# Four gated-merge blocks beside the last mixer head, another handover from the up- to the down-projection, and the last rows' Newton steps on VectorE

## The chip, the cores and the metric

The kernel runs on one core of a Trainium2 chip. The metric is the device time of one execution in microseconds (us). Engines are named as in the profile: PE is the matmul engine (TensorE), PEld its weight load, DVE is VectorE, ACT is ScalarE, POOL is GpSimd, SP issues the DMAs.

## The reference: one transformer-like layer for two request groups

A prompt of 1024 tokens and 8 samples of 16 new tokens (1152 tokens together, float32, model width 1024) pass one layer. Three mixers A (sliding-window attention), B (gated linear recurrence, 4 heads) and C (gated DeltaNet, 4 heads) are merged with gates; a feed-forward of width 2816 follows.

```python
offsets = [int(o) for o in np.cumsum(IN_SPLITS)[:-1]]
aq, ak, av, bq, bf, bi, bg, cqkv, cz, cb, ca, gt = jnp.split(x @ w_in, offsets, axis=-1)
...
o_b, new_hgrn = run_chunks(gla_chunk, s_hgrn.astype(F32), (q_b, k_b, v_b, log_f))
o_b = merge_heads(rms_norm_gated(o_b, hgrn_w, heads(bg, B_VAL_DIM)))
...
gates = jax.nn.sigmoid(gt.reshape(bsz, t, N_BRANCH, D_MODEL))
w_ba, w_bb, w_bc = jnp.split(w_branch, [A_WIDTH, A_WIDTH + B_WIDTH], axis=0)
mix = gates[:, :, 0] * (o_a @ w_ba) + gates[:, :, 1] * (o_b @ w_bb) + gates[:, :, 2] * (o_c @ w_bc)
x = layer_norm(ALPHA * x + mix @ w_out, ln1_g, ln1_b)

up, new_ffn_conv = causal_dwconv(x @ w_up, buf_ffn, f_conv_w)
gate, val = jnp.split(up + f_conv_b, 2, axis=-1)
x = layer_norm(ALPHA * x + (jax.nn.silu(gate) * val) @ w_down, ln2_g, ln2_b)
```

`causal_dwconv` is a convolution over three tokens in each channel; `rms_norm_gated` divides a head's output by its root mean square, multiplies by a weight and by silu of a gate z.

## The kernel before

**Numbers and tiles.** Tokens lie in three row blocks n = 0, 1, 2 of 384 (`NW`); block 2 holds the last 256 prompt tokens and the 128 sample tokens. A matrix product keeps both operands as a high part (a CAST to the matmul's reduced float32, written fp32r in the profile) and a low part (the rest, one DVE subtraction), and sums three products: high x high, high x low, low x high. So each weight tile costs one load by SP, one ACT CAST and one DVE subtraction (`prep`, `pair`, `prep_step`), and each product tile three matmuls, all issued from `mm` at L108. `block` makes one 128 x 384 output from `kt` tiles of the contraction, and then calls its eviction.

**What sets the order.** The program is written as one sequence, with generators beside it: `beside(gen)` enters one, `tick()` inside the matmul loops steps those whose count has run down, a `yield k` waits k ticks, and `drain()` ticks until none is left. The compiler schedules the emitted instructions engine by engine, by the order of emission and by priorities, and may move them by its own estimate; `keep_in_program_order` and `load_in_turn` bind an instruction to its place. Each engine, and SP's list of DMA issues, then runs its list in order. Tiles come from pools with a number of buffers for each tag; a new tile waits until the old one's readers are done.

**The end of the mixers and the merge.** The 24 groups of mixer work (head, row block) run as generators beside the matmuls. The last is head 3 of B with n = 2: `b_finish` computes a mean square `so`, `rsqrt` makes its inverse root on DVE by an integer guess and three Newton steps (L319 to L327, 2 + 9 instructions), and `finish_group` multiplies the head's output oT by it (L703), transposes its three pieces on PE, multiplies with the weight and z into the tile sq (L709), and stores that to DRAM as d_o. `load_o` reads d_o again and splits it into o high and low (L1478, L1479). The merge multiplies d_o of each branch with its rows of w_branch; `branch_ev` multiplies by the gates and adds into `mix` (L1517, L1518). Branches 2 and 0 run in a queue `Q` beside the mixers. Branch 1 (mixer B) is last: `whl_pair` fetches the weights of the output rows m = 0..3 into two whl buffers, and two more pairs go into wres buffers (raw in wraw). Before, `drain()` stands ahead of all of this, and a loop over n and m then makes the 24 blocks of branch 1, each with `kt=4`, 12 matmuls.

**The up-projection.** 22 pairs of weight columns, a gate and a value column block each (`Pair`). For pairs 2 to 21 the 2 x 2 pattern (two halves of the contraction) x (row blocks 0 and 1) is made by a Strassen-like scheme: seven products over sums of x and of the weights, where `x_sums` builds the four sums of x in four tiles ts. `put` brings a product into xp, `conv` applies the three taps, and the result goes to DRAM as d_gu. Row block 2 is made by plain blocks (`gate_rest`, `behind`). The last transposes of each pair (tile l, `tail`) give the convolution's new state.

**The down-projection.** `prep_step` is one of 66 steps: for n = 0 one weight row block (wdr, CAST L1957, subtraction L1958), and the features of one k: two loads from d_gu (gr), their product (L1962), CAST (L1965) and subtraction (L1966) into gd. The contraction of 22 is done in two halves of 11 k for each n; each step is 18 matmuls of 512 columns into six PSUM banks. `residual` loads the normalised rows into nine tiles yac, times g plus b of the first layer norm (L1943, L1944); `put_sum` adds each half into yac (L2054), `last_ln` does the final layer norm. For the last 128 rows it runs on DVE, with `rsqrt_act`, in which the nine Newton operations are ACT instructions (L1993 to L1996).

The pools: wp holds wraw and whl (2 buffers each, 8 and 16 KB), s0 the 48 tiles of x high and low, xs the sums ts; dp, which is opened after all of these are closed, holds the down-projection's tiles.

## Time and profile before

| what | us |
|---|---|
| three runs | 2266.27, 2268.82, 2265.26 |
| their median | 2266.27 |
| the profiled execution, in all | 2266.73 |
| its span on the profile's page | 2264.9 |

The page gives the busy time of each engine and its share of the span; a digit of the lines by slices is the busy share of one fortieth of the span in tenths. The table of waits counts idle time of one engine by the operation and tile that waited and by what ended the wait: total, times, longest. A row of the timeline is a group of like instructions: start, length, engine, line, operation, out<-in, shape, count, and in brackets the idle time ahead of it with its releaser. A row by stretches has its window and length, then the busy time of PE, PEld, DVE, ACT and POOL, the granted PE clock, the share of the DMA engines and GB/s. The page's lines on the DMA queues give packets, MB and a share of the time of the core's 16 DMA engines; one queue carries nearly everything:

```profile
q1 hardware_dynamic: 261200, 218.06, 31.1%
```

### The profile page before, as it was taken

The numbers are of one execution on the slowest core, as the hardware profiler recorded it, in microseconds if no ns is written. First come the engines' busy times: TensorE is split into PE (matmuls) and PEld (weight loads), VectorE is DVE, ScalarE is ACT, GpSimd is POOL, SyncE is SP. The second block draws the span as 40 slices with busy tenths as digits, with TensorE's granted clock in tenths as the row PEclk, the third lists the DMA queues.
The fourth block names the chain that finished last, engine by engine and source line by source line (L and its number), as shares of the span: only waits on it lengthen the run. The fifth ranks groups of instructions, "written<-read, shape, count | busy, mean of one in ns | idle before, by whom it ended". The sixth has DMA issues, their size and how long they took to land.

```text
span 2264.9 us, 35159 instructions
## 1 busy us (share of the span) xinstructions
PE 2178.8 (96%) x12759; PEld 2030.1 (90%) x12759; DVE 1530.2 (68%) x4246; ACT 982.7 (43%) x2309; POOL 1.3 (0%) x9
## 2 busy tenths in 40 slices
PE   7999999999999999999999899999999999689998
PEld 7998889999999999999989888899999999567886
DVE  7367556666765657767878786877777777674444
ACT  4356434344345346355433333544545445231234
POOL 0000000000000000000000000000000000000000
PEclk9999999999999999999999999999999999899999
DMA  5121231222222221312354541232323232674421
GB/s 139 44 76 56 86 102 48 74 73 65 69 78 57 76 60 52 94 42 64 119 157 137 164 151 75 70 102 94 102 97 108 92 97 76 224 233 128 155 98 56
DMA packets 261373, 220.30 MB, mean 97 GB/s; under 512 B 38810, under 2 KB 250688, under 8 KB 261184
## 3 DMA queue, kind: packets, MB, share of 16 engines
q1 hardware_dynamic: 261200, 218.06, 31.1%
q8 instruction: 100, 1.64, 0.3%
q14 instruction: 73, 0.60, 0.1%
HBM read 152.86 MB, written 66.06 MB: 97 GB/s over the span
## 4 chain that ended last, share of the span: by engine, by line
PE 85%; DVE 5%; DMA 5%; ACT 3%; issue 1%; SPq 1%; DVEq 0%; ACTq 0%
PE psg L108 72%; PE psp L108 5%; PE psch L108 4%; DMA gr<-d_gu 2%; PE psp L148 2%; PE psch L148 1%; PE psms L108 1%; PE psms L148 1%; DMA xp<-d_o 1%; SPq L111 1%; DVE gr L1962 0%; DVE yac L1944 0%; DVE gd L1966 0%; ACT L1223 0%; DVE yac L1943 0%
## 5 line engine op out<-in xcount | busy, mean ns | idle before, releaser
L108 PE MATMUL psg<-hh,whl 128*128 128x384 f32 x2976 | 809.0, 344 | 0.8 <-ACT qf L436 0.7
L108 PEld LDWEIGHTS psg<-hh,whl 128*128 128x128 f32 x2976 | 535.6, 188 | 15.4 <-issue 8.6
L108 PE MATMUL psg<-hl,whl 128*128 128x384 f32 x1488 | 508.5, 342 | 0.0
L108 PE MATMUL psg<-wd,gd 128*128 128x512 f32 x1188 | 277.0, 396 | 30.9 <-ACT gd L1965 11.2
L108 PEld LDWEIGHTS psg<-wd,gd 128*128 128x128 f32 x1188 | 227.1, 192 | 80.6 <-ACT gd L1965 11.4
L108 PEld LDWEIGHTS psg<-hl,whl 128*128 128x128 f32 x1488 | 280.1, 188 | 4.3 <-issue 2.6
L108 PE MATMUL psg<-x1h,w 128*128 128x384 f32 x672 | 182.0, 340 | 0.0
L108 PE MATMUL psg<-x1h,whl 128*128 128x384 f32 x640 | 172.7, 339 | 2.8 <-ACT whl L212 1.2
L108 PE MATMUL psg<-o,whl 128*128 128x384 f32 x720 | 142.8, 349 | 6.6 <-ACT o L1478 2.6
L108 PEld LDWEIGHTS psg<-o,whl 128*128 128x128 f32 x720 | 127.3, 194 | 9.8 <-ACT o L1478 3.2
L108 PEld LDWEIGHTS psg<-x1h,w 128*128 128x128 f32 x672 | 122.9, 188 | 1.0
L108 PEld LDWEIGHTS psg<-x1h,whl 128*128 128x128 f32 x640 | 116.9, 189 | 4.9 <-ACT whl L212 1.9
L108 PE MATMUL psg<-x1l,w 128*128 128x384 f32 x336 | 113.5, 338 | 0.0
L213 DVE TENSOR_TENSOR whl<-wraw,whl 128x1024 fp32r<-128x1024 f32 (+1 forms) x82 | 91.5, 1117 | 31.9 <-ACT whl L212 30.8
L108 PE MATMUL psg<-x1l,whl 128*128 128x384 f32 x320 | 108.2, 338 | 0.0
L108 PE MATMUL psg<-ts,w 128*128 128x384 f32 x576 | 105.8, 334 | 0.0
L108 PEld LDWEIGHTS psg<-ts,w 128*128 128x128 f32 x576 | 100.6, 188 | 0.0
L1962 DVE TENSOR_TENSOR gr<-gr 128x384 f32<-128x384 f32 x66 | 36.7, 557 | 92.7 <-DMA gr<-d_gu 92.2
L212 ACT CAST whl<-wraw 128x1024 fp32r<-128x1024 f32 (+1 forms) x82 | 79.0, 964 | 36.8 <-PE psg L108 34.4
L108 PE MATMUL psg<-wres,mixh 128*128 128x512 f32 x288 | 92.5, 395 | 0.0
L1965 ACT CAST gd<-gr 128x384 fp32r<-128x384 f32 x66 | 33.8, 512 | 129.5 <-PE psg L108 78.3
L1445 ACT ACTIVATE ga<-psg 128x384 f32<-128x384 f32 x72 | 35.4, 491 | 97.6 <-PE psg L108 80.0
(505 smaller groups left out, 3829.1 us busy)
## 6 DMA issues: line engine op xcount, KB each, us to landing
wraw<-in_w_in_dram SPq DMA_DIRECT2D x58, 512.0 KB
gr<-d_gu SPq DMA_DIRECT2D x132, 192.0 KB
d_g<-ga SPq DMA_DIRECT2D x72, 192.0 KB
wraw<-in_w_up_dram SPq DMA_DIRECT2D x24, 512.0 KB
wdr<-in_w_down_dram SPq DMA_DIRECT2D x22, 512.0 KB
wr<-in_w_up_dram SPq DMA_DIRECT2D x20, 512.0 KB
acc<-d_g SPq DMA_DIRECT2D x48, 192.0 KB
d_gu<-ga SPq DMA_DIRECT2D x44, 192.0 KB
```

The lines of the kernel that those rows point to most:

```text
L108: PE.matmul(out, lhsT, rhs, start=start, stop=stop)
L111: nc.sync.dma_start(out=out, in_=in_)
L148: PE.transpose(out, in_, ident[:n, :n])
L212: S.copy(hl[:, 0, :kt, :cols], raw[:, :kt, :cols])
L213: V.tensor_sub(hl[:, 1, :kt, :cols], raw[:, :kt, :cols], hl[:, 0, :kt, :cols].bitcast(F32))
L1445: S.activation(g, ps, AF.Tanh, scale=0.5)
L1962: V.tensor_mul(raw[:, 0], raw[:, 0], raw[:, 1])
L1965: S.copy(g[:, 0], raw)
```

## The change

**Part 1: the merge beside the last head's close.** The program no longer drains ahead of branch 1. It ticks until the last group has computed its mean square (`ended`), prepares the two whl pairs, runs the four blocks m = 0..3 of n = 0, and only then drains. `finish_group` waits 10 ticks in place of 2 for this last group, and its first transpose keeps its place in the program. The loop leaves out the four blocks done; the gate tiles fetched ahead are those of m = 4..6.

```diff
-    def finish_group(oT, fac, wcol, z2, out):
+    def finish_group(oT, fac, wcol, z2, out, behind=False):
 
         V.tensor_mul(u3(oT), u3(oT), bc(fac, 3))
-        yield 2
+        yield 10 if behind else 2
         ps = psum("ms")
         for i in range(3):
-            tr(ps[:, i * P:(i + 1) * P], oT[:, i * P:(i + 1) * P])
+            t = PE.transpose(ps[:, i * P:(i + 1) * P], oT[:, i * P:(i + 1) * P], ident)
+            if behind and i == 0:
+                tc.keep_in_program_order(t)
...
-    drain()
+    while not ended[0]:
+        tick()
...
     whl_pair(2)
+
+    oh, ol, _ = parts[1]
+    for m in range(4):
+        block(wb[m], oh, ol, 0, branch_ev(1, m), kt=4)
+    drain()
     mix_ctx.close()
...
-    for m in range(3):
+    for m in range(4, 7):
         gate_ahead[1, m, 0] = load_gate(1, m, 0)
...
+            if n == 0 and i < 4:
+                continue
```

PE's list at the end of branch 0, before: the last matmuls of branch 0 (onto whl_14385), the transposes of the last head's oT, and the first matmuls of branch 1 (onto whl_14439).

```order
L108 MATMUL psg_14526<-o_13769,whl_14385 128x384
L108 MATMUL psg_14526<-o_13770,whl_14385 128x384
L108 MATMUL psg_14526<-o_13769,whl_14385 128x384
L148 MATMUL psms_14348<-call,oT_14211 128x128 x3
L108 MATMUL psg_14601<-o_14463,whl_14439 128x384
L108 MATMUL psg_14601<-o_14464,whl_14439 128x384
```

And now, 48 matmuls later: the fourth block of branch 1 (onto whl_14567), the transposes, and the first matmuls onto the wres pairs.

```order
L108 MATMUL psg_14623<-o_14481,whl_14567 128x384
L108 MATMUL psg_14623<-o_14482,whl_14567 128x384
L108 MATMUL psg_14623<-o_14481,whl_14567 128x384
L707 MATMUL psms_14422<-call,oT_14211 128x128 x3
L108 MATMUL psg_14669<-o_14463,wres_14658 128x384
L108 MATMUL psg_14669<-o_14464,wres_14658 128x384
L108 MATMUL psg_14685<-o_14463,wres_14658 128x384
```

The transposes have moved from ahead of the four whl blocks to behind them. DVE's list at the same place, before: the last eviction of branch 0 (L1518), the Newton steps, the scaling of oT and the write of sq.

```order
L1518 TENSOR_TENSOR mix_12588<-mix_12588,acc_14539 128x384
L324 TENSOR_TENSOR nwa_14315<-nwi_14312 128x3
L325 SCALAR_TENSOR_TENSOR nwa_14315<-nwa_14315,rq_3024_14297 128x3
L327 SCALAR_TENSOR_TENSOR nwy_14318<-nwa_14315,nwi_14312 128x3
L324 TENSOR_TENSOR nwa_14320<-nwy_14318 128x3
L325 SCALAR_TENSOR_TENSOR nwa_14320<-nwa_14320,rq_3024_14297 128x3
L327 SCALAR_TENSOR_TENSOR nwy_14323<-nwa_14320,nwy_14318 128x3
```

And now, from the second of these Newton operations to the seventh:

```order
L325 SCALAR_TENSOR_TENSOR nwa_14315<-nwa_14315,rq_3024_14297 128x3
L1522 SCALAR_TENSOR_TENSOR acc_14619<-acc_14619,psg_14606 128x384
L1523 TENSOR_TENSOR mix_12568<-mix_12568,acc_14602 128x384
L327 SCALAR_TENSOR_TENSOR nwy_14318<-nwa_14315,nwi_14312 128x3
L1523 TENSOR_TENSOR mix_12571<-mix_12571,acc_14619 128x384
L324 TENSOR_TENSOR nwa_14320<-nwy_14318 128x3
L1522 SCALAR_TENSOR_TENSOR acc_14636<-acc_14636,psg_14623 128x384
L325 SCALAR_TENSOR_TENSOR nwa_14320<-nwa_14320,rq_3024_14297 128x3
L1523 TENSOR_TENSOR mix_12574<-mix_12574,acc_14636 128x384
L327 SCALAR_TENSOR_TENSOR nwy_14323<-nwa_14320,nwy_14318 128x3
L324 TENSOR_TENSOR nwa_14325<-nwy_14323 128x3
```

The scaling of oT (L703) stands three rows further. The evictions of the four blocks stand among the Newton steps now. ACT's list, with the changed kernel's lines, has behind them:

```order
L1483 CAST o_14563<-z_14561 128x384
L1572 CAST wres_14658<-wraw_14659 128x1024
L1572 CAST wres_14663<-wraw_14664 128x1024
```

The CAST of the reloaded z is ahead of the two CASTs of wres, as it was before (at L1478 and L1566).

**Part 2: the handover to the down-projection.** The Strassen scheme takes row block 1 where it took 0 and the reverse, so that x high and low of block 0, k < 4, are read for the last time by `x_sums`, and their s0 buffers come free. Four feature steps of the down-projection are prepared ahead of the up-projection's last two blocks (now in `ending`): raw features in freed s0 pieces, results in one tile g4 that takes the place of a ts tile; two weight steps in whl buffers. The pool wp stays open, so that raw weights go on through its wraw buffers; weights 2 and 3 follow right after. The nine tiles yac become three tiles of three rows in the ts buffers. `residual(n)` loads and treats three rows for each row block, with loads bound to their place, and `put_sum` has a priority. gr has 2 buffers in place of 3, gd 12 (and 4 in g4) in place of 13, wd 10 (and 2 in whl) in place of 12. `tail` waits 10 ticks in place of 5.

```diff
-        pr.put(0, 0, product(pr.a1, 1, B21), p1)
-        pr.conv(0, 0)
+        pr.put(0, 1, product(pr.a1, 1, B21), p1)
...
-    gate_rest()
-    behind()
-
+
+    def ending():
+        gate_rest()
+        behind()
...
+    EARLY = 4
+    g4 = quarter_of_xs("g4")
+    for s in range(EARLY):
+        if s < 2:
+            prep_weights(s)
+        prep_features(0, s, [s0_piece("gr", F32) for _ in range(2)], g4[:, 0, s], g4[:, 1, s])
+    ahead[0] = EARLY
+    ending()
     drain()
-    xs_ctx.close()
     late.close()
     s0_ctx.close()
-    wp_ctx.close()
...
+    yac = []
+    for n in range(NBLK):
+        y3 = quarter_of_xs("yac").bitcast(F32).rearrange("p a b c -> p (a b c)")
+        yac += [y3[:, i * D:(i + 1) * D] for i in range(3)]
+    for k in range(2, EARLY):
+        prep_weights(k)
...
-        for j in range(NT):
-            load(yac[j], d_xn1[j * P:(j + 1) * P, :])
-            yield 3
+        for j in range(3 * n, 3 * n + 3):
+            load_in_turn(yac[j], d_xn1[j * P:(j + 1) * P, :])
+            yield 4
             V.tensor_mul(yac[j], yac[j], gb[:, 0])
             V.tensor_add(yac[j], yac[j], gb[:, 1])
-            yield 3
+            yield 1
...
     def put_sum(half, j, hf, ps):
-        if half == 0 or j == NT - 1:
...
+        with tc.high_priority(60):
+            if half == 0 or j == NT - 1:
...
-            if (half, n) == (0, 0):
-                prepare(3)
-                beside(residual())
+            if half == 0:
+                beside(residual(n), 12 if n == 0 else 1)
...
-                    prepare(min(at + 8, 3 + 2 * at))
+                    prepare(at + 8 if at > 1 else at + 6 + at)
```

PE's list at the handover, before: the last matmul of the up-projection, the last transpose of l, and the first matmuls of the down-projection, onto wd and gd.

```order
L108 MATMUL psg_21596<-x1h_16180,w_4210_21427 128x384
L148 MATMUL psms_21635<-call,l_4231_21584 36x128
L108 MATMUL psg_21704<-wd_21670,gd_21677 128x512
L108 MATMUL psg_21705<-wd_21670,gd_21677 128x512
L108 MATMUL psg_21706<-wd_21670,gd_21677 128x512
```

And now, where the first operands are whl_21557 and g4:

```order
L108 MATMUL psg_21635<-x1h_16180,w_4214_21427 128x384
L148 MATMUL psms_21674<-call,l_4248_21623 36x128
L108 MATMUL psg_21707<-whl_21557,g_4233_21555 128x512 x3
L108 MATMUL psg_21708<-whl_21557,g_4233_21555 128x512 x3
L108 MATMUL psg_21709<-whl_21557,g_4233_21555 128x512 x3
```

The place of the transposes is the same; what the matmuls behind them read has changed. DVE's list in the up-projection's last convolutions (L1782, L1785) now holds the subtractions of the early features:

```order
L1959 TENSOR_TENSOR g_4233_21555<-gr_21561,g_4233_21555 128x384
L1785 SCALAR_TENSOR_TENSOR va_21492<-xp_21489,fvec,va_21492 128x384
L1782 SCALAR_TENSOR_TENSOR ga_21521<-xp_21518,fvec,ga_21521 128x384
L1756 TENSOR_TENSOR xp_21547<-psg_21534,u_4216_21431 128x384
L1777 COPY xp_21619<-xp_21472 128x2
L1782 SCALAR_TENSOR_TENSOR ga_21528<-xp_21472,fvec,ga_21528 128x384
L1959 TENSOR_TENSOR g_4233_21555<-gr_21573,g_4233_21555 128x384
```

They stood behind the last convolution before, as L1966.

**Part 3: the last rows' Newton steps.** In `last_ln` of the last 128 rows, `rsqrt_act` gives way to `rsqrt`, whose eleven operations are all DVE's.

```diff
-                rs = rsqrt_act(var)
+                rs = rsqrt(dp, var, 1)
```

More of the change, by code (lines that the diff above doesn't have):

```diff
@@ L1432, in b_group @@
         done[0] += 1
-    done = [0]
+    done, ended = [0], [False]
     GT = 4872
@@ L1914, in tile_encoder_step @@
             gate_rest()
-            next(parts_[i + 1])
-        pr.put(1, 0, product(pr.a2, 1, T4), u3)
-        pr.conv(1, 0)
+            next(parts_[i + 1], None)
+        pr.put(1, 1, product(pr.a2, 1, T4), u3)
         pr.conv(1, 1)
-    gate_rest()
-    behind()
+    def ending():
+        gate_rest()
+        behind()
+    raw_w = lambda: wp.tile([P, D], F32, tag="wraw", name=nm("wraw"), bufs=2)
+    two_w = turn(*2 * [lambda: wp.tile([P, 2, D], F32R, tag="whl", name=nm("whl"), bufs=2)],
+                 *10 * [lambda: dp.tile([P, 2, D], F32R, tag="wd", name=nm("wd"), bufs=10)])
@@ new lines, in tile_encoder_step, with prep_weights, prep_features @@
+    wd, gd = {}, {}
+    rows_of = [range(0, NFF // 2), range(NFF // 2, NFF)]
+    steps = [(half, n, k) for half in range(2) for n in range(NBLK) for k in rows_of[half]]
+    ahead = [0]
+    def prep_weights(k):
+        raw, hl = raw_w(), two_w()
+        load(raw, w_down[0, k * P:(k + 1) * P, :])
+        S.copy(hl[:, 0], raw)
+        V.tensor_sub(hl[:, 1], raw, hl[:, 0].bitcast(F32))
+        wd[k] = hl
+    def prep_features(n, k, raw, gh, gl):
+        for half in range(2):
+            load(raw[half], d_gu[half][k][:, tok(n)])
+        V.tensor_mul(raw[0], raw[0], raw[1])
+        S.copy(gh, raw[0])
+        V.tensor_sub(gl, raw[0], gh.bitcast(F32))
+        gd[k, n] = gh, gl
@@ L1930, in tile_encoder_step @@
-    yac = [yp.tile([P, D], F32, name=f"yac{j}") for j in range(NT)]
-    wd, gd = {}, {}
-    late_w = lambda: dp.tile([P, 2, D], F32R, tag="wd", name=nm("wd"), bufs=12)
-    def residual():
-        gb = dp.tile([P, 2, D], F32, name="gb2")
-        for i, src in enumerate((ln1_g[0], ln1_b[0])):
-            load(gb[:, i], src.partition_broadcast(P))
-        yield 6
-        S.mul(gb, gb, ALPHA)
-        for j in range(NT):
-            load(yac[j], d_xn1[j * P:(j + 1) * P, :])
-            yield 3
+    yac = []
@@ new lines, in tile_encoder_step, with residual @@
+    for n in range(NBLK):
[3 more added lines that the diff above has]
+        prep_weights(k)
+    gb = dp.tile([P, 2, D], F32, name="gb2")
+    def residual(n):
+        if n == 0:
+            for i, src in enumerate((ln1_g[0], ln1_b[0])):
+                load_in_turn(gb[:, i], src.partition_broadcast(P))
+            S.mul(gb, gb, ALPHA)
+            yield 2
+        for j in range(3 * n, 3 * n + 3):
+            load_in_turn(yac[j], d_xn1[j * P:(j + 1) * P, :])
+            yield 4
@@ L1968, in terms @@
+        if n == NBLK - 1:
+            for t, src in enumerate((ln2_g, ln2_b)):
+                load_in_turn(gb[:, t], src[0].partition_broadcast(P))
+    def prep_step(half, n, k):
+        if n == 0 and k not in wd:
+            prep_weights(k)
+        raw = dp.tile([P, 2, NW], F32, tag="gr", name=nm("gr"), bufs=2)
+        g = dp.tile([P, 2, NW], F32R, tag="gd", name=nm("gd"), bufs=12)
+        prep_features(n, k, [raw[:, i] for i in range(2)], g[:, 0], g[:, 1])
     def terms(ps, k, n, i, cs, first, stop):
-        g, sl = gd[k, n], slice(i * P, (i + 1) * P)
@@ L2042, in tile_encoder_step @@
     cols = [slice(hf * 512, (hf + 1) * 512) for hf in range(2)]
-    rows_of = [range(0, NFF // 2), range(NFF // 2, NFF)]
-    steps = [(half, n, k) for half in range(2) for n in range(NBLK) for k in rows_of[half]]
-    ahead = [0]
     def prepare(upto):
@@ L2087, in tile_encoder_step @@
     drain()
+    late.close()
     xs_ctx.close()
-    late.close()
+    wp_ctx.close()
     banks["ctx"].close()
```

61 lines of the change are left out of this document (24 added, 37 removed).

## The prediction

> **What bounds the kernel now.** I read the page first, then the waits of the matmul engine PE, then its timeline where the long waits lie.
>
> ```profile
> span 2264.9 us, 35159 instructions
> ...
> PE 2178.8 (96%) x12759; PEld 2030.1 (90%) x12759; DVE 1530.2 (68%) x4246; ACT 982.7 (43%) x2309; POOL 1.3 (0%) x9
> ...
> PE   7999999999999999999999899999999999689998
> ```
>
> These are the span, the busy time by engine and the span in 40 slices of 56.6 us. PE is busy in 9 tenths or more of nearly every slice. So an edit is worth what it takes out of PE's idle time, plus what follows PE's last matmul; the only slice below 8, the first apart, is number 35 (counted from 1), about 1925 to 1982 us, where the up-projection hands over to the down-projection.
>
> ```profile
> PE psg L108 <- ACT gd L1965: 11.2, 1, 11.2
> PE psg L108 <- DVE gd L1966: 8.3, 1, 8.3
> ...
> PE psg L108 <- DVE wd L1958: 7.8, 1, 7.8
> PE psms L148 <- DVE oT L703: 7.1, 1, 7.1
> PE psg L108 <- DVE yac L2054: 3.7, 2, 1.9
> ...
> PE psg L108 <- DVE x L1517: 2.4, 2, 1.8
> ```
>
> This is who PE waited for, in us, times and longest. The first three rows and the fifth are of the down-projection, the fourth is the end of the last mixer head, the last row is the merge of that branch. Together they are 40.5 us, and the edits lie at exactly these places.
>
> **The merge beside the last head's close.** PE's timeline there (start, length, matmuls, idle before):
>
> ```profile
> 1245.14 2.16 PE L108 MATMUL psg<-o,whl 128*128 128x384 f32 x11
> 1254.43 0.88 PE L148 MATMUL psms<-call,oT 128*128 128x128 f32 x3 [7.13 <-DVE oT L703]
> 1254.96 11.10 PE L108 MATMUL psg<-o,whl 128*128 128x384 f32 x48
> 1265.90 8.48 PE L108 MATMUL psg<-o,wres 128*128 128x384 f32 x48
> ```
>
> PE ends the branch-0 blocks at 1247.30, idles 7.13, does three transposes of oT, and then runs the four n = 0 blocks of branch 1 whose weights are already in place: 48 matmuls from 1254.96 to 1265.90. The next 48 take 8.48 by the timeline where these took 11.10, so the first 48 lose 2.62 us to a slow clock:
>
> ```profile
> 1256.00:1258.00 2.00, 2.00 (x8) 2.00 (x8) 0.00 (x0) 0.00 (x0) 0.00 (x0) 0.50 0.30 107
> ...
> 1260.00:1262.00 2.00, 2.00 (x12) 2.00 (x11) 0.56 (x1) 1.41 (x3) 0.00 (x0) 0.88 0.93 278
> ```
>
> (columns: stretch, length, busy of PE, PEld, DVE, ACT, POOL, granted clock, DMA share, GB/s). The granted clock is 0.50 from the end of the hole and full some six us later.
>
> What the hole waits for is VectorE (DVE):
>
> ```profile
> 1251.50 0.55 DVE L1518 TENSOR_TENSOR mix<-mix,acc 128x384 f32<-128x384 f32 x1
> 1251.97 0.15 DVE L324 TENSOR_TENSOR nwa<-nwi 128x3 f32<-128x3 f32 x1
> ...
> 1253.73 0.56 DVE L703 TENSOR_TENSOR oT<-oT,nwy 128x384 f32<-128x384 f32 x1
> 1255.35 0.62 DVE L709 SCALAR_TENSOR_TENSOR sq<-psms,vec,z 128x384 f32<-128x384 f32 x1 [1.06 <-PE psms L148]
> ```
>
> Nine Newton operations stand between 1251.97 and 1253.73, 0.195 us each, then the scaling of oT; the transposes follow 0.14 after its end, and sq 0.92 after their start. Behind that come SP's store and the reload, and ScalarE's (ACT's) two kinds of CAST:
>
> ```profile
> 1251.15 0.38 SPq L111 DMA_DIRECT2D wraw<-in_w_branch_dram  x1
> 1255.99 0.32 SPq L111 DMA_DIRECT2D d_o<-sq  x1
> 1258.29 0.32 SPq L111 DMA_DIRECT2D z<-d_o  x1
> ```
>
> ```profile
> 1260.59 0.51 ACT L1478 CAST o<-z 128x384 fp32r<-128x384 f32 x1 [11.80 <-DMA z<-d_o]
> 1261.01 2.00 ACT L1566 CAST wres<-wraw 128x1024 fp32r<-128x1024 f32 x2
> ```
>
> From sq's end (1255.97) the store is issued after 0.02, the reload of z 2.30 later, its CAST 2.30 after that, and only then the two CASTs of wres, 1.05 each: the first ends at 1262.06, 7.63 us after the transposes began. The raw weights of wres were asked for by 1251.15; ACT comes to them late because the CAST of z stands ahead of them in its list. The 10.94 us of the four blocks lie over exactly this chain, and nothing waits for wres.
>
> The change puts those 48 matmuls into the hole. At full clock they take 8.32, from 1247.30 to 1255.62. But their four evictions (two operations each, 0.47 apart) now stand in DVE's list between the Newton operations. Worked forward row by row from 1251.50, the last of the four blocks, ready at about 1255.8, is evicted at 1255.85; five more small operations and the scaling put the end of oT at 1258.35. So the transposes start at about 1258.5, PE having idled 2.9. Then the chain of 7.63 has no matmul beside it: ACT's list still has the CAST of z ahead of wres, and the next matmul needs wres. wres's first half is there at 1266.1. PE idles 6.8 again and starts at the slow clock.
>
> From there 240 matmuls of the merge are left at 8.32 / 48 = 0.173, 41.6 us. Before, the same 240 started at 1265.90 warm and lost 2.4 to the row of x. After: 0.2 later, plus 2.0 of slow clock (the resumptions of this trace lost 1.5 to 2.6, the others below), less what the later PE no longer waits for x. I keep 1.0 of those 2.4, since DVE has four evictions less to do after the hole, and DVE is full there. 0.2 + 2.0 - 1.4: **+0.8 us**, bounds -0.7 (no wait for x left, clock loss 1.5) and +4 (reload and casts each a little longer, all of the waits stay). The gate loads of the first four row blocks go ahead of the store in SP's list; SP is free between 1251.53 and 1255.99, so they hold nothing.
>
> [...]
>
> **The start of the down-projection.** PE's timeline, the group of all its matmuls on the page, and a stretch of it without any wait (PE alone: busy, count, clock, DMA share, GB/s):
>
> ```profile
> 1945.80 0.29 PE L148 MATMUL psms<-call,l 128*36 128x128 f32 x1 [0.87 <-ACT l L1753]
> 1957.29 12.54 PE L108 MATMUL psg<-wd,gd 128*128 128x512 f32 x48 [11.20 <-ACT gd L1965]
> 1977.59 4.45 PE L108 MATMUL psg<-wd,gd 128*128 128x512 f32 x12 [7.76 <-DVE wd L1958]
> 1990.35 19.82 PE L108 MATMUL psg<-wd,gd 128*128 128x512 f32 x78 [8.31 <-DVE gd L1966]
> ```
>
> ```profile
> L108 PE MATMUL psg<-wd,gd 128*128 128x512 f32 x1188 | 277.0, 396 | 30.9 <-ACT gd L1965 11.2
> ```
>
> ```profile
> 2100.00:2200.00 100.00, 100.00 (x443) 1.00 0.40 130
> ```
>
> After the up-projection's last transpose (ending 1946.09) PE waits 11.20 for the first operands, 7.76 for the second weights' low half and 8.31 for features. 100 us hold 443 matmuls including those cut at the ends, so 0.2262 us each; all 1188 are 268.8. They took 277.0, so 8.2 is slow clock after the holes, and 30.9 is idle. All that could be won here is 39.1 us.
>
> The change makes four feature steps and two weight steps ready before, and starts two more weight loads. Four steps are 72 matmuls, 16.3 us: PE is supplied from 1946.1 to 1962.4. Steps two and three need only a CAST and a subtraction behind the last convolution. The fifth step needs a load issued after the last store:
>
> ```profile
> 1949.71 0.34 SPq L111 DMA_DIRECT2D d_gu<-gv  x1
> ...
> 1952.77 0.43 SPq L111 DMA_DIRECT2D wdr<-in_w_down_dram  x1
> ```
>
> ```profile
> 1958.19 1.05 ACT L1957 CAST wd<-wdr 128x1024 fp32r<-128x1024 f32 x1 [0.95 <-DMA wdr<-in_w_down_dram]
> ```
>
> The last store goes out at 1949.71. Before, the second weight load was issued at 1952.77 and its CAST began 5.42 later; with 1.05 for the CAST and 1.2 for the subtraction a load at the same place is usable at about 1960.5, two us before PE asks. Every later step takes PE 18 x 0.2262 = 4.07, and the pair of raw buffers gives two weights in about 7 to 8. I count the start at nothing, covered by the four early steps; without that cover it costs the 11.2 again.
>
> The 8.31 had another cause:
>
> ```profile
> 1982.93 6.89 DVE L1944 TENSOR_TENSOR yac<-yac,gb 128x1024 f32<-128x1024 f32 x6
> 1989.74 0.55 DVE L1966 TENSOR_TENSOR gd<-gr,gd 128x384 fp32r<-128x384 f32 x1
> ```
>
> DVE multiplied and added the residual rows in a run (these six end a set of eighteen) while the low half of a feature step waited behind them. After, three rows are loaded and treated for each row block, spread over ticks, and the eviction into yac gets priority; this removes 8.3, and the yac waits of 3.7. The buffers for raw features fall from 3 to 2: each cycle of load and three operations is about 4.7 us for two steps, under PE's 8.1, hidden by PE. Three residual rows in one tile add no operation.
>
> What can still be late is the last residual row: seven steps of 0.92 MB, the vectors and rows of 2.6 and the next features of 1.6 are 10.6 MB in the 36.5 us from 1950.5 to the first change of row block at 1987:
>
> ```profile
> 2000.00:2020.00 20.00, 20.00 (x90) 16.54 (x89) 15.25 (x23) 9.45 (x14) 0.00 (x0) 1.00 0.90 296
> ```
>
> That needs 290 GB/s, and this stretch moved 296. So I leave 1.1 for it: **-38.0 us**, bounds -39.1 and -29 (a tenth less than 290 is 4 us, twice that and the slow clock behind it 10).
>
> **The up-projection** gets eight feature loads, four products, four CASTs and subtractions, and two weight loads, all moved forward:
>
> ```profile
> 1600.00:1700.00 100.00, 100.00 (x576) 99.58 (x576) 77.41 (x151) 49.20 (x107) 0.00 (x0) 1.00 0.29 94
> ```
>
> DVE is busy 77 of 100 us here and PE is never idle; 4 x 1.1 us of DVE fit. The row blocks change places with equal counts. Four of the loads wait in SP's list for a store to land, some 2.3 as above, and hold the weight loads behind them. The waits for the transposes of l (0.87 ahead of 1945.80) stay, since the drain still emits it. I take **+0.3**, bounds -1 and +3.
>
> **The last block's Newton steps.**
>
> ```profile
> 2257.28 0.14 DVE L1986 TENSOR_SCALAR nwi<-lnvr 128x1 int32<-128x1 int32 x1
> ...
> 2260.59 1.54 DVE L2020 SCALAR_TENSOR_TENSOR yac<-yac,nwy,gb 128x384 f32<-128x384 f32 x3 [2.98 <-ACT nwy L1996]
> ```
>
> From the first of them to the final scaling 3.31 us pass, through nine ACT operations. After, two and nine operations run on DVE at 0.195, 2.15. **-1.15 us**, bounds -0.9 and -1.4.
>
> **Sum.** +0.8 - 38.0 + 0.3 - 1.15 = -38.05. The profiled execution took 2266.73 in all (span 2264.9 and 1.8 around it), 0.46 above the median of 2266.27: 2228.7 against it, and **2228.5 us** against the median to the nearest half.
>
> **Rivals.** (A) The merge does what its name says: ACT is not held by z, or PE finds other work, and only the 2.9 stays. Then part one is 2.9 - 7.13 - 2.62 = -6.9 and the time 2221. Against it: the CAST order, and an ACT that idled 11.8 us for z with wres's raw weights asked for. 9 in 100. (B) The down-projection's start is starved after all: the transfers run at 225 to 260 GB/s, as stretches with small gaps would, and the first change of row block, or steps five to seven, wait 6 to 12 with the clock: 2234 to 2240. For it: the need of 290 beside 296. Against it: four steps of lead. 17 in 100. (C) Slower: in the up-projection SP, held by the early loads, brings weights late and DVE stops on the products. Ten moved loads, each with a store's landing and its own, 4.6 us, would be 46: 2274. It decides from 3.8 us of PE per load on. Against it: PE has seven banks, waits nowhere between 1500 and 1940, and DVE has 23 us in 100 free. 3 in 100. (D) Gain and new waits cancel within 0.2%: 2 in 100. The forecast (2226 to 2233) has 69.
>
> The range 2221 to 2240 takes in A's end, most of B and the bounds above. A difference of about 0.2% (4.5 us) is what a measurement of this kernel can tell from no change. Faster by more: 0.95, within: 0.02, slower: 0.03.
>
> **What would show it.** Right: PE's idle before the transposes of oT about 3 and a second hole of 6 to 7 between them and the first matmul on wres, with ACT waiting for z; no PE wait over 2 us between 1946 and the end, and about 45 us for the first row block; the three small waits on yac gone; 2.1 us from the first Newton row to the last scaling. Wrong: wres cast before z; waits of PE on wd, gd or yac at the start; PE waits in the up-projection; a total outside -29 to -46.

## The result, and the profile after

| | median us | runs | ratio to before |
|---|---|---|---|
| before, with a fourth run | 2266.38 | 2265.26 to 2268.82 | |
| the changed kernel | 2244.79 | 2243.72 to 2246.85 | 0.9904 [0.9887, 0.9922] |

The change saves 21.6 us; 38 were forecast, and the time lies above the range. The profiled execution took 2245.31, its span is 2243.5. The lines of its page that answer to those of before:

```profile
span 2243.5 us, 35145 instructions
...
PE 2181.5 (97%) x12759; PEld 2026.7 (90%) x12759; DVE 1533.2 (68%) x4254; ACT 975.1 (43%) x2300; POOL 1.3 (0%) x9
...
PE   7999989999999999999999899999999999999998
```

The slice of the handover, number 35, is full now. But PE's busy time has risen by 2.7 us, though its matmuls are the same 12759 and the three cold stretches behind the old holes of the handover (granted clock 0.50, 27.3 us together by the clock records, idle time included) are gone. That is the first sign of what failed. PE's waits, from the table of waits of the changed kernel (us, times, longest):

```profile
PE psg L108 <- DVE yac L2089: 6.5, 2, 4.1
PE psg L108 <- ACT wres L1572: 6.4, 1, 6.4
...
PE psms L707 <- DVE oT L703: 2.6, 1, 2.6
...
PE psg L108 <- DVE x L1522: 0.8, 1, 0.8
```

The waits for wd and gd are gone from the table. The waits for yac, the evictions of the down-projection (now L2089), have grown from 3.7 to 6.5, and a wait for wres has come.

Cut at the first matmul of each stage, the two traces differ so (us):

| stage | before | after | difference | predicted |
|---|---|---|---|---|
| to the last matmul of branch 0 | 1247.14 | 1245.49 | -1.65 | 0 |
| merge, to the first matmul of the output projection | 63.30 | 63.15 | -0.15 | +0.8 |
| output projection, to the first matmul on ts | 172.02 | 173.70 | +1.7 | } +0.3 |
| rest of the up-projection, to the last transpose of l | 463.35 | 463.88 | +0.5 | |
| down-projection | 308.01 | 287.37 | **-20.6** | -38.0 |
| last layer norm | 11.14 | 9.95 | -1.19 | -1.15 |

Five of the six lie within 2 us of the forecast; the down-projection is 17.4 short. Its timeline on PE (start, length, matmuls, idle before):

```profile
1946.25 8.68 PE L108 MATMUL psg<-whl,g 128*128 128x512 f32 x36
1954.77 8.56 PE L108 MATMUL psg<-wd,g 128*128 128x512 f32 x36
1963.17 29.56 PE L108 MATMUL psg<-wd,gd 128*128 128x512 f32 x126
1992.57 2.73 PE L108 MATMUL psg<-whl,gd 128*128 128x512 f32 x11
1997.70 7.65 PE L108 MATMUL psg<-whl,gd 128*128 128x512 f32 x25 [2.40 <-DVE yac L2089]
...
2050.08 7.32 PE L108 MATMUL psg<-whl,gd 128*128 128x512 f32 x24 [4.12 <-DVE yac L2089]
...
2107.64 35.16 PE L108 MATMUL psg<-wd,gd 128*128 128x512 f32 x150
2142.64 1.10 PE L108 MATMUL psg<-whl,gd 128*128 128x512 f32 x4
```

The four early steps (x36 and x36) run without a hole, and so does the rest of the first row block: 198 matmuls from 1946.25 to 1992.57. But 150 matmuls of a stretch without a wait now take 2142.64 - 2107.64 = 35.0 us, 0.2333 each at a granted clock of 1.00; this time from one matmul's start to the next is called the pitch here. The prediction took 0.2262 for it, so over 1188 matmuls 8.4 us are missing. (The starts of before's single matmuls give a finer pitch of 0.2267; against that the rise is 6.67 ns, 7.9 us in all.) The waits for yac are 6.5. The clock is low there, at 0.50 for 3.41 us each: the x25 take 7.49 us to the next group in place of 5.83, the x24 take 7.16 in place of 5.60, 3.2 together. 8.4 + 6.5 + 3.2 is 18.1; the forecast had left 1.1 for a late row, so 17.0 of the 17.4 are found. The experiments ask where these terms come from.

### The profile page after: what moved, and what is told of

It is laid out like the page before. It is cut to its first block, busy times and chain, and to the rows that moved or that the text cites. A ratio compares the mean times of both kernels' runs of the same rounds, so it can differ in the third digit from the quotient of the medians.

```text
span 2243.5 us, 35145 instructions
## 1 busy us (share of the span) xinstructions
PE 2181.5 (97%) x12759; PEld 2026.7 (90%) x12759; DVE 1533.2 (68%) x4254; ACT 975.1 (43%) x2300; POOL 1.3 (0%) x9
## 4 chain that ended last, share of the span: by engine, by line
PE 87%; DVE 4%; DMA 4%; ACT 3%; issue 1%; SPq 0%; DVEq 0%; ACTq 0%
PE psg L108 74%; PE psp L108 5%; PE psch L108 4%; PE psp L148 2%; DMA gr<-d_gu 1%; PE psch L148 1%; PE psms L108 1%; DMA wraw<-in_w_out_dram 1%; DMA yac<-d_xn 1%; SPq L111 0%; ACT L1225 0%; PE psms L148 0%; DVE gr L1957 0%; PE psms L707 0%; DMA gb<-in_ln_b_dram 0%
## 5 line engine op out<-in xcount | busy, mean ns | idle before, releaser
L108 PE MATMUL psg<-wd,gd 128*128 128x512 f32 x936 | 220.8, 396 | 0.0
L108 PEld LDWEIGHTS psg<-wd,gd 128*128 128x128 f32 x936 | 175.8, 188 | 42.6
L1779 ACT ACTIVATE va<-xp,fvec 128x384 f32<-128x384 f32 (+1 forms) x66 | 47.1, 716 | 84.2 <-DVE xp L1775 83.9
```

What stands on the lines that cost most here:

```text
L108: PE.matmul(out, lhsT, rhs, start=start, stop=stop)
L1779: S.activation(acc[:, :w], xp[:, 2:2 + w], AF.Identity, scale=fvec[:, 2, ct:ct + 1], bias=fvec[:, 3, ct:ct + 1])
```

## The experiments

**Why is each matmul 6.67 ns longer?** The instruction is the same. The one thing that I found changed is where the tiles lie: in the built programs the moving operand (wd, or whl for two k of each half) and the weights loaded from gd begin at these addresses, modulo 256 bytes: before, wd 128 and gd 128; after, wd and whl 96, gd 128, the four early features 224. The rival was absolute: a place of its own that is slow. Two kernels, the first from the changed one, the second from before:

```diff
-                mv = dp.tile([P, 1, 2], F32, tag="lnmv", name=nm("lnmv"), bufs=3)
-                st = dp.tile([P, 2, 6], F32, tag="lnst", name=nm("lnst"), bufs=3)
+                mv = dp.tile([P, 1, 2], F32, tag="lnmv", name=nm("lnmv"), bufs=1)
+                st = dp.tile([P, 2, 6], F32, tag="lnst", name=nm("lnst"), bufs=1)
...
-    three_halves = dp.tile([P, 1], F32, name="three_halves")
+    three_halves = dp.tile([P, 64], F32, name="three_halves")[:, :1]
```

> The changed kernel; only the tiles' places differ: one small tile of the down-projection's pool is made 256 bytes long, so that gd begins at 96 modulo 256 bytes as wd and whl do (before this edit gd begins at 128, wd and whl at 96; in the kernel before the change wd and gd both begin at 128). Theory OFFSET (the down-projection's matmuls got slower, 226.7 to 233.3 ns, because weights and moving operand no longer begin at the same address modulo 256): the 1116 matmuls on gd take 226.7 ns again, the first 72, on g4 at 224, stay at 233.3; the down-projection is 7.4 us shorter and the time about 2237.4. Rival ABSOLUTE (wd as the moving operand must begin at a multiple of 64 bytes): wd has not moved, so 233.3 ns stays and the time is that of the changed kernel, 2244.8. Rival ORDER OR LOAD (more traffic or another order of the matmuls slows them): no change either.

```diff
+        if (half, n, k) == (0, 0, 0):
+            V.memset(dp.tile([P, 1], F32, name="gap"), 0.0)
         raw = dp.tile([P, 2, NW], F32, tag="gr", name=nm("gr"), bufs=3)
```

> The kernel before the change with a tile of 32 bytes between wd and gd (and one small memset), so that gd begins at 160 modulo 256 and wd stays at 128. Theory OFFSET: all 1188 matmuls of the down-projection take 233.3 ns in place of 226.7, so the time rises by 7.9 us less what the waits there absorb: the first three holes wait for data and absorb some, so +6 to +8, about 2273. Rivals ABSOLUTE (wd unmoved) and ORDER OR LOAD: no change, 2266.3.

The first puts gd at 96 like wd and whl, the second moves gd of before to 160 and leaves wd at 128. offset_equal, PE's timeline:

```profile
1962.65 28.72 PE L108 MATMUL psg<-wd,gd 128*128 128x512 f32 x126
...
2104.45 34.16 PE L108 MATMUL psg<-wd,gd 128*128 128x512 f32 x150
2138.45 1.07 PE L108 MATMUL psg<-whl,gd 128*128 128x512 f32 x4
```

The same 150 take 34.0 us, 0.2267 each, the pitch of before; the down-projection fell from 287.4 to 281.1, and the time was 2238.76 us, ratio 0.9882 [0.9865, 0.9899]; that interval overlaps the changed kernel's, so the pitch and the stage carry the reading, not the whole time. 1116 matmuls at 6.67 ns are 7.4 (the 72 on the early features keep their distance), of which longer waits for yac, 7.9 in place of 6.5, took 1.4 back. And before_gap32, then before, the last long group of PE's timeline:

```profile
2075.46 182.72 PE L108 MATMUL psg<-wd,gd 128*128 128x512 f32 x782 [1.25 <-DVE yac L2056]
```

```profile
2074.85 179.17 PE L108 MATMUL psg<-wd,gd 128*128 128x512 f32 x782 [1.90 <-DVE yac L2054]
```

The group of before holds about 1.7 us of slow clock behind its longer wait, so the two lengths differ by less than the pitch. A stretch without a wait shows it better: 100 us held 443 matmuls before, by the row in the prediction, and hold 430 with the gap:

```profile
2100.00:2200.00 100.00, 100.00 (x430) 80.50 (x430) 48.29 (x106) 30.79 (x69) 0.00 (x0) 1.00 0.41 132
```

A gap of 32 bytes that holds nothing of use costs 5.1 us: 2271.39, ratio 1.0025 [1.0015, 1.0034], the down-projection 313.25 in place of 308.01. That is less than 1188 x 6.67 ns = 7.9, as the waits of that stage differ too (12.8 in place of 11.2 for the first operands, 4.8 in place of 7.8 for the second weights). wd stood at the same place in both, so the absolute place is not it: the distance is. How does it go with the distance? Each of 13 gd buffers 32 bytes further from wd than the last, in before:

```diff
-        g = gd[k, n] = dp.tile([P, 2, NW], F32R, tag="gd", name=nm("gd"), bufs=13)
+        g = dp.tile([P, 2 * NW + 8], F32R, tag="gd", name=nm("gd"), bufs=13)
+        g = gd[k, n] = g[:, :2 * NW].rearrange("p (a w) -> p a w", a=2)
```

> The kernel before the change with the thirteen buffers of gd 3104 bytes apart in place of 3072, so that their starts differ from wd's by 0, 32, 64, ... 384 bytes modulo 512, one for each step in turn. Theory OFFSET modulo 256: steps whose buffer begins at a distance of 0 or 256 take 226.7 ns a matmul, all others 230 to 234. If only 64 bytes matter, every second buffer (distances 0, 64, 128, ...) is fast; if nothing but a whole 512 counts, the one at distance 0 alone. About eleven of thirteen steps slow would make the whole 4 to 7 us longer than before, 2270 to 2273.

Mean time from one matmul's start to the next, from the trace's records, by the distance of gd from wd modulo 512 bytes, over the steps ahead of the last row block that use one buffer throughout and have no wait and no slow clock in them (three to five steps for each distance):

```
bytes     0    32    64    96   128   160   192   224   256   288   320   352   384
ns    227.0 233.2 233.4 233.9 232.0 233.5 229.1 233.4 227.6 233.3 233.5 234.1 232.8
```

Equal starts are fastest, and 256 is near them: two of its three steps took 226.6 and 226.7, the third 229.4. 192 costs 2 ns, every other distance 5 to 7. The time, 2271.7 in one run, is that of the gap. Why the distance counts was not shown.

**Whose are the waits for yac?** The prediction gave the evictions to the residual rows and let the smaller pair of raw feature buffers be free. One kernel for each, then both:

```diff
-            if half == 0:
-                beside(residual(n), 12 if n == 0 else 1)
+            if half == 0 and n < 2:
+                if n == 0:
+                    beside(residual(0), 1)
+                beside(residual(n + 1), 12 if n == 0 else 1)
```

> The changed kernel, with the residual rows of each row block asked for one row block earlier: those of blocks 0 and 1 during block 0, those of block 2 during block 1. Theory LATE ROWS (the evictions into yac stand in VectorE's list behind the rows' products, whose loads are bound to their place behind the feature loads of eight steps ahead and so land at the very end of a block): the two waits of the matmul engine on yac, 6.5 us, go, and the slow clock after them, about 3; time about 2235.5. Rival TWO BUFFERS (the evictions wait because VectorE stands at a feature product whose load was late, as raw features have two buffers in place of three): the waits stay, 5 to 7 us, time 2243 to 2246. A first block that starves on the earlier transfers would show as waits on wd or gd between 1946 and 1990 and make it slower than 2245.

```diff
-        raw = dp.tile([P, 2, NW], F32, tag="gr", name=nm("gr"), bufs=2)
-        g = dp.tile([P, 2, NW], F32R, tag="gd", name=nm("gd"), bufs=12)
+        raw = dp.tile([P, 2, NW], F32, tag="gr", name=nm("gr"), bufs=3)
+        g = dp.tile([P, 2, NW], F32R, tag="gd", name=nm("gd"), bufs=11)
```

> The changed kernel with three buffers for raw features, as before the change, in place of two, and eleven for gd in place of twelve, to keep the size. In the run with the rows asked for early the first wait on yac went and the second, 5.3 us, stayed: there VectorE stood at feature products whose loads SP had issued late, as a buffer was not free. Theory TWO BUFFERS: with three the feature steps run ahead of the list's evictions, the second wait falls under 2 us, the first, which has late rows as its cause, may stay at 2 to 3; time about 2240. Rival LIST ORDER (the evictions stand in VectorE's list behind too many steps, whatever the buffers): both waits stay, 6 to 8 us, 2243 to 2246.

> The changed kernel with both edits, the residual rows asked for one row block earlier and three buffers for raw features (eleven for gd). If the first wait on yac comes from late rows and the second from two buffers, no wait on yac over 1 us is left and the slow clock behind them goes, together 8 to 10 us: about 2236. If LIST ORDER holds, a wait of 4 to 6 us stays and the time is 2240 to 2244.

| kernel | waits for yac | down-projection | median us | ratio |
|---|---|---|---|---|
| changed kernel | 2.40 + 4.12 | 287.37 | 2244.79 | 0.9904 [0.9887, 0.9922] |
| rows_early | 5.33 | 284.21 | 2243.45 | 0.9895 [0.9881, 0.9910] |
| gr_three | 1.41 + 1.75 | 282.47 | 2240.45 | 0.9887 [0.9872, 0.9902] |
| rows_early_gr_three | 2.50 + 0.98 | 281.51 | 2240.26 | 0.9891 [0.9875, 0.9908] |

The intervals of the ratios overlap; it is the segment and the waits that carry this. Rows treated earlier take away the first wait and not the second. DVE's timeline in rows_early ahead of the second, where no row is left:

```profile
2034.86 0.56 DVE L1957 TENSOR_TENSOR gr<-gr 128x384 f32<-128x384 f32 x1 [2.36 <-DMA gr<-d_gu]
2036.59 0.56 DVE L1957 TENSOR_TENSOR gr<-gr 128x384 f32<-128x384 f32 x1 [1.17 <-DMA gr<-d_gu]
2037.06 0.55 DVE L1959 TENSOR_TENSOR gd<-gr,gd 128x384 fp32r<-128x384 f32 x1
2037.80 0.56 DVE L1959 TENSOR_TENSOR gd<-gr,gd 128x384 fp32r<-128x384 f32 x1 [0.19 <-ACT gd L1958]
2040.64 0.56 DVE L1957 TENSOR_TENSOR gr<-gr 128x384 f32<-128x384 f32 x1 [2.28 <-DMA gr<-d_gu]
2042.51 0.56 DVE L1957 TENSOR_TENSOR gr<-gr 128x384 f32<-128x384 f32 x1 [1.31 <-DMA gr<-d_gu]
2042.98 0.55 DVE L1959 TENSOR_TENSOR gd<-gr,gd 128x384 fp32r<-128x384 f32 x1
2043.72 0.56 DVE L1959 TENSOR_TENSOR gd<-gr,gd 128x384 fp32r<-128x384 f32 x1 [0.19 <-ACT gd L1958]
2044.20 1.88 DVE L2089 TENSOR_TENSOR yac<-yac,psg 128x512 f32<-128x512 f32 x3
```

PE stops at about 2039.6 and waits 5.33 for an eviction into yac. The evictions stand in DVE's list behind two more products of features, which wait 2.28 and 1.31 for their loads; with two raw buffers two steps take 5.8 us a round (2034.86 to 2040.64). What DVE waited for between 2024 and 2048 (us, times, longest), in the changed kernel and then in gr_three:

```profile
DVE gr L1957 <- DMA gr<-d_gu: 5.8, 4, 2.0
DVE gd L1959 <- ACT gd L1958: 4.6, 7, 0.7
DVE yac L1992 <- DMA yac<-d_xn: 0.5, 1, 0.5
```

```profile
DVE gr L1957 <- DMA gr<-d_gu: 3.5, 2, 3.0
DVE yac L1992 <- DMA yac<-d_xn: 3.1, 3, 1.2
```

The third buffer takes 10.9 us of idle time to 6.6, the waits for the CAST of a step above all, as another step's product is at hand then. The evictions come earlier: five of them from 2041.86 in gr_three, two from 2049.34 in the changed kernel. Where the rows are early, the third buffer halves the second wait too (5.33 to 2.50, with a new one of 0.98), though DVE's idle time on loads in that stretch is nearly the same (11.8 and 11.3); why the wait falls there is less plain, and the 2236 expected of both edits together did not come. With three buffers the waits are 3.2, about the 3.7 before the change. So at this pitch the pair of buffers is half of the 6.5, and the rows and the priority together removed next to nothing of the old 3.7. This share holds at the slow pitch only: with the short matmuls of offset_equal the waits are 7.9, and the third buffer, in the last kernel below, takes them only to 6.4. What else holds the evictions there stays open.

**Do the four early steps carry the gain at the start?** First the early steps written behind the last convolutions in place of ahead of them:

```diff
+    ending()
     EARLY = 4
...
     ahead[0] = EARLY
-    ending()
     drain()
```

> The changed kernel with the last two blocks of the up-projection written ahead of the four early feature steps and the two early weights, so that these are loaded only behind the last stores. Theory COVER (the early steps are what closed the first holes of the down-projection): PE waits 8 to 12 us for the first operands after the last transpose, at the slow clock behind it, and perhaps again for later steps; the down-projection takes 300 to 312 us in place of 287.4, time 2258 to 2270. Rival (the raw buffers kept open and the shared pools closed the holes, not the early steps): a first wait under 4 us and a time below 2252.

2247.62, two runs, the down-projection 286.85: no change. But this doesn't tell the theories apart, as SP's list shows the same issues in the same order at the end (the second of the down-projection's weights at 1909.85 there, 1909.03 in the changed kernel): the scheduler had put the loads early again. So one feature step was made early in place of four. (The loop then holds only one of the two early weight steps, but SP's list has the loads of the down-projection's weights at 1907.77, 1925.69 and 1929.48, as far ahead of the handover as the 1909.03, 1926.94 and 1930.74 of the changed kernel.)

```diff
-    EARLY = 4
+    EARLY = 1
```

> The changed kernel with one feature step made ahead of the handover instead of four (EARLY = 1; the first two weights stay early). If the four early steps are the cover that closed the holes of the start: PE has 18 matmuls, 4.1 us, from 1946.3 to 1950.3; the next features, asked for behind the last store as those of the fifth step were in the changed kernel, are ready about 1956.0 as those were; so a PE wait of about 5.7 on gd, then a slow clock of about 2.6, perhaps one more wait behind: down-projection 295 (292 to 299) in place of 286.8 to 287.4, time 2253 (2250 to 2257). Rival, the holes were closed by buffers that come free earlier and by the order of SP's list alone, the early steps add nothing: no new PE wait over 2 us, time 2243 to 2247.

2249.97, ratio 0.9935 [0.9915, 0.9955]; the down-projection 292.52. PE's timeline in early_one:

```profile
1945.00 4.48 PE L108 MATMUL psg<-whl,g 128*128 128x512 f32 x18
1952.18 2.16 PE L108 MATMUL psg<-whl,gd 128*128 128x512 f32 x6 [2.70 <-ACT gd L1958]
1954.57 3.94 PE L108 MATMUL psg<-whl,gd 128*128 128x512 f32 x12 [0.22 <-DVE gd L1959]
...
2004.53 7.31 PE L108 MATMUL psg<-whl,gd 128*128 128x512 f32 x24 [4.68 <-DVE yac L2089]
...
2056.29 4.21 PE L108 MATMUL psg<-whl,gd 128*128 128x512 f32 x9 [6.08 <-DVE yac L2089]
...
2152.11 7.63 PE L108 MATMUL psg<-whl,gd 128*128 128x512 f32 x32
2159.58 33.51 PE L108 MATMUL psg<-wd,gd 128*128 128x512 f32 x147
2192.93 1.56 PE L108 MATMUL psg<-whl,gd 128*128 128x512 f32 x6
```

The cover counts, though not as sized: the wait at the start is 2.9, not 5.7, because PE began when ACT's CAST was there (after 2.70, and 0.22 more for DVE's subtraction), and the lateness comes out behind it, as 10.8 for yac in place of 6.5. An accident confirms the distance: in this kernel's pools gd and wd both start at 128, whl at 96. So in one stage of one kernel the 32 matmuls on whl take 7.47 us, 0.2334 each, and the 147 on wd 33.35, 0.2269. 972 faster matmuls give 6.5 back; without them the stage would have been 299.0, so three early steps are worth about 11.6 us, a figure that takes the yac waits as the same at either pitch.

**The new hole of the merge.** It was predicted; is it the CAST of z? In z_late the last tile is reloaded into a buffer of its own behind the wres pairs, and its CAST stands behind theirs; in z_late_after_blocks its CAST and subtraction stand eight blocks later (after m = 7 of n = 0):

```diff
-            for k in range(4):
+            for k in range(3 if (br, n) == (1, NBLK - 1) else 4):
...
     for m in (4, 6):
         pair(m, mp.tile([P, 2, 4, 2 * P], F32R, tag="wres", name=nm("wres"), bufs=8))
+    zr = mr.tile([P, NW], F32, name="zlast")
+    load(zr, d_o[1][3 * P:4 * P, tok(NBLK - 1)])
+    oh[3][NBLK - 1], ol[3][NBLK - 1] = s0_piece("o"), s0_piece("o")
+    tc.keep_in_program_order(S.copy(oh[3][NBLK - 1], zr))
+    V.tensor_sub(ol[3][NBLK - 1], zr, oh[3][NBLK - 1].bitcast(F32))
```

> The changed kernel, with the last piece of the last head's output (z) reloaded into a tile of its own and cast behind the two CASTs of wres on ScalarE. Theory CAST ORDER (the second hole, 6.4 us, is ScalarE standing at the CAST of z while wres's raw weights lie ready): wres is cast before the transposes, the matmul engine goes from the transposes straight on, and the hole goes together with the 2.3 us of slow clock behind it, less up to 2 us for the low part of wres, which still follows sq on VectorE: time about 2238 to 2240. Rival RAW WEIGHTS (wres's weights arrive no earlier than z): the hole stays above 5 us and the time at 2243 to 2246.

> The changed kernel with z's reload in a tile of its own, and both parts of its split, the CAST on ScalarE and the subtraction on VectorE, bound behind the eight blocks of n = 0. In the run z_late the hole of 6.4 us went, but VectorE stood 6.0 us at z's subtraction, ahead of the evictions, and the matmul engine then waited 5.5 in five places on x. Theory CAST ORDER: with that subtraction out of the way the waits on x fall to what they were (0.8 to 2.4), the merge from the end of branch 0 to the first matmul of the output projection takes 55 to 57 us in place of 63.0, and the time is about 2238.5. Rival FULL VECTORE (VectorE cannot evict and split faster than that, whatever the order): the waits on x stay above 4 us and the merge above 60.

z_late, 2242.29, 0.9891 [0.9876, 0.9906], rows of its timeline:

```profile
1251.71 1.05 ACT L1572 CAST wres<-wraw 128x1024 fp32r<-128x1024 f32 x1 [4.78 <-DMA wraw<-in_w_branch_dram]
...
1264.85 0.56 DVE L1607 TENSOR_TENSOR o<-zlast,o 128x384 fp32r<-128x384 f32 x1 [6.03 <-ACT o L1606]
```

wres is cast before z now, and the hole of 6.40 is gone, so that was its cause. But the wait moved on: DVE stood 6.03 on z's subtraction, and PE waited 5.5 for x later. The merge took 62.3, 0.9 less than in the changed kernel. z_late_after_blocks, 2243.07, 0.9900 [0.9886, 0.9915], merge 60.8, PE's timeline and the stretch behind (columns as in the prediction):

```profile
1258.42 0.52 PE L707 MATMUL psms<-call,oT 128*128 128x128 f32 x3 [2.58 <-DVE oT L703]
1258.70 10.44 PE L108 MATMUL psg<-o,wres 128*128 128x384 f32 x48
...
1296.19 4.19 PE L108 MATMUL psg<-o,whl 128*128 128x384 f32 x15 [2.08 <-DVE x L1522]
```

```profile
1260.00:1262.00 2.00, 1.87 (x7) 1.36 (x6) 1.86 (x2) 0.00 (x0) 0.00 (x0) 0.50 0.66 200
1262.00:1264.00 2.00, 2.00 (x10) 2.00 (x9) 0.04 (x1) 0.00 (x0) 0.00 (x0) 0.68 0.84 251
```

PE goes straight on after the transposes, yet the 48 matmuls still take 10.44 in place of 8.48, since the clock fell to 0.50 behind a hole of 2.58. (In z_late 40 matmuls behind the same hole took 7.24, 0.181 each, with no slow stretch to be seen.) PE being earlier, it waits 3.9 for x, where DVE is the later one; the 55 to 57 us expected of the CAST order alone did not come.

**Two last kernels**: the three edits that helped (offset_equal, gr_three, z_late_after_blocks) together, and the changed kernel once more.

> The changed kernel with three of the edits together: gd at the same distance modulo 256 as wd and whl, three raw feature buffers, and z split behind the eight blocks. From the segments of the runs alone: the down-projection 287.4 less 6.3 (distance) less 4.9 (buffers) gives 276; the merge 63.2 less 2.3 gives 61; the rest as in the changed kernel, with 1.7 open either way for the clock at the start of the up-projection. If the edits add up, the time is 2231 (2229 to 2234). If the shorter matmuls let the evictions run late again, the waits on yac rise above 5 us and the time is 2235 or more.

> The changed kernel itself, on the same chip as the others of this call, for the sizes: 2244.8 (2243 to 2247), with 6 to 7 us of waits on yac, 6.4 on wres and 233.3 ns a matmul in the down-projection; the segment between the first matmul of the output projection and the first on the sums of x is 172.0 or 173.7, as the clock drops there or not.

The three together took 2234.18 (2231.57 to 2235.7), ratio 0.9855 [0.9839, 0.9871], 32 us under before and below the changed kernel's interval. It is the fastest version found. Its down-projection is 280.6, not much under the 281.1 of the equal starts alone: with shorter matmuls PE is earlier at the evictions, and the waits for yac are back at 3.46 and 2.96. The changed kernel again took 2246.21, 0.9910 [0.9896, 0.9924]; its merge was 66.56 in place of 63.15 and its output projection 171.96 in place of 173.70. The profiled runs of all kernels show how far these two stages vary. Where the merge is the changed one, seven of eight traces have 62.8 to 63.2 and this one 66.56; so the 60.8 of z_late_after_blocks, with 60.6 in the three together, lies below all of them, while the 62.3 of z_late is hardly apart. The output projection took 172.0 to 175.4 in the eleven traces with the change and 171.8 to 172.0 in the three without it; the clock's part in that is taken up below.

## Why the prediction was wrong, point by point

- **The pitch of a matmul.** "1188 are 268.8 ... all that could be won here is 39.1 us" carried 0.2262 us from the trace of before to the changed kernel. That is the step that failed first: the pitch went with where before's tiles happened to lie, wd and gd both at 128. With the tiles of the changed kernel elsewhere, at 96 and 128, each matmul took 0.2333, 8.4 us more in all than the sum had (7.9 by the finer pitch), shown from both sides (offset_equal, before_gap32) and within one kernel (early_one). No rival had it, since none asked what a new tile does to the addresses of the others. The trace of before, read with the addresses of its program, could have told: its matmuls of 384 columns followed one another every 174.1 ns where both operands start equal modulo 256 bytes, and every 176.0 where they start 128 apart.
- **"the eviction into yac gets priority; this removes 8.3, and the yac waits of 3.7".** The 8.3 went. The 3.7 did not: 6.5 were measured, in two waits of 2.40 and 4.12 where the signs allowed none over 2. The evictions still stand in DVE's list behind products that wait for loads (2.28 and 1.31 in the rows of rows_early above); what the priority alone does was not tried.
- **"The buffers for raw features fall from 3 to 2 ... hidden by PE".** On the mean rate that is so; but at the change of row block DVE's list is what PE waits for, and there the missing buffer cost half of the 6.5 and, with the clock behind it, 4.9 (gr_three). The round of two steps, put at 4.7, took 5.8.
- **The clock.** The slow clock behind the old holes, 8.2 by the prediction's pitch and 7.7 by the finer one, went; 3.2 came back behind the new ones, twice 3.41 us at 0.50, which the sum did not have.
- **The start of the down-projection** was right: no wait from 1946 to the end of the first row block, 46.3 us where 45 were forecast, the difference being the pitch. That the four steps are the cover is shown (11.6 us for three of them). Of rival B the starving didn't come; that its time, 2234 to 2240, is the nearer one is luck.
- **The merge**: +0.8 forecast, -0.15 measured, in a stage where one trace in eight lay 3 us off. The mechanism came as told: 2.58 idle ahead of the transposes, 6.40 behind them, and ACT's list with z ahead of wres:

```profile
1261.97 0.51 ACT L1483 CAST o<-z 128x384 fp32r<-128x384 f32 x1 [14.82 <-DMA z<-d_o]
1262.39 1.99 ACT L1572 CAST wres<-wraw 128x1024 fp32r<-128x1024 f32 x2
```

  Rival A's -6.9 would not have come with the CASTs in the other order either: in z_late_after_blocks the merge is 60.8, 2.5 less than before the change, and DVE and the clock kept the rest.
- **The up-projection**: +0.3 forecast. +0.5 came in the stage of the moved loads. The +1.7 ahead of it is no cost of theirs: it follows the clock at 1480, where the same two waits (1.77 and 0.48) left it at 1.00 before and at 0.50 after, for 3.41 us from 1479.90, and the repeat of the changed kernel doesn't have it.
- **Two slips of the prediction** change nothing: 2266.27 - 38.05 is 2228.2, to the nearest half 2228.0 and not 2228.5, and the signs name three waits on yac where the table has two.
- **The Newton steps** were right: from the first row to the last scaling 2.12 us, 2.15 forecast:

```profile
2237.05 0.15 DVE L319 TENSOR_SCALAR nwi<-lnvr 128x1 int32<-128x1 int32 x1
...
2239.17 1.54 DVE L2058 SCALAR_TENSOR_TENSOR yac<-yac,nwy,gb 128x384 f32<-128x384 f32 x3
```

## What to carry to other kernels

Before a duration is carried from the trace of one kernel to another, ask what it depends on that the change touches. Here it was where the tiles lie: with gd 32 bytes from wd modulo 256, in place of none, a matmul of 512 columns took 6.67 ns longer, so where tiles are added to a pool, compare such start addresses before and after. In rows_early the evictions into yac stood in DVE's list behind two products that waited 2.28 and 1.31 us for their loads, and PE waited 5.33: a buffer that is idle on the mean may be what keeps an eviction in time. An edit that closes a hole is worth what the next engine in line lets through: here the parts, each good for 2 to 6 us, gave together less than their sum.

## What the runs showed of the hardware

- Matmuls of 512 columns (fp32r) followed one another every 227 ns in before, where wd, which PE streams, and gd, which it loads as weights, start at the same address modulo 256 bytes, and every 233 ns in the changed kernel, where they start 32 apart. In offset_scan it was 227.0 at equal starts, 227.6 at a distance of 256 (one step of three was slower), and 232.0 to 234.1 at the other distances up to 384 in steps of 32 bytes, but for 229.1 at 192. The matmuls of 384 columns in the two kernels of the change show the same: 174.1 at a distance of 0, and 176.0 to 176.1 at 128.
- In the changed kernel's down-projection the granted clock fell to 0.50 at 1998.72, 1.02 us after the hole of 2.40 had ended, and at 2049.92, 0.16 before the one of 4.12 ended, and stayed low for 3.41 us each time, by the clock records of the trace. It fell to 0.50 behind the hole of 2.58 in z_late_after_blocks too. In the traces of the two kernels of the change every low stretch, but for the one that the end cuts off, lasts 3.41, 6.83 or 10.24 us, and the low stretches of one trace begin whole multiples of 3.413 us apart; in the changed kernel, for example, at 1438.94, 1479.90, 1998.72 and 2049.92. The stretches behind the 2.40, by windows:

```profile
1998.00:2000.00 2.00, 2.00 (x7) 1.53 (x7) 2.00 (x4) 0.52 (x1) 0.00 (x0) 0.68 0.08 30
2000.00:2002.00 2.00, 2.00 (x6) 1.58 (x5) 2.00 (x5) 0.37 (x1) 0.00 (x0) 0.50 0.02 4
2002.00:2004.00 2.00, 2.00 (x9) 1.57 (x9) 1.65 (x3) 0.14 (x1) 0.00 (x0) 0.97 0.46 130
```

  The length of a hole alone did not tell whether the clock fell: behind one pair of waits (1.77 and 0.48) it stayed at 1.00 before and fell to 0.50 after, and behind a hole of 2.58 in the merge it fell in z_late_after_blocks (48 matmuls in 10.44) and, by the length of its matmuls, not in z_late (40 in 7.24).
